# FFN2's down projection: the eleventh pair of inner tiles goes through the seven products as well, and the output is stored block by block

## The chip, the cores and the metric

The kernel runs on one core of a Trainium2 chip. The metric is the device time of one execution in microseconds. The core's engines work side by side, each through its own list of instructions in order: TensorE (PE in the profile, its weight loads PEld), VectorE (DVE), ScalarE (ACT), GpSimd (POOL) and SyncE (SP, its DMA queue SPq). All transfers of this kernel are issued by SyncE.

## The reference

One layer of a decoder trunk: a half-step SwiGLU feed-forward (FFN1), a mixing block of two attentions, and a second half-step SwiGLU (FFN2). Only the last one matters here:

```python
def swiglu(x, w_gate, w_up, w_down):
    return (jax.nn.silu(x @ w_gate) * (x @ w_up)) @ w_down

x = x + FFN_RESIDUAL_WEIGHT * swiglu(rms_norm(x, ffn2_norm[l]),
                                     ffn2_w_gate[l], ffn2_w_up[l], ffn2_w_down[l])
```

There are 1024 tokens, the model width is 1024, the hidden width is 2816, and the factor is 0.5. The last product is therefore [1024, 2816] by [2816, 1024], in float32.

## The kernel before

The hidden width is cut into 22 inner tiles of 128. Each float32 operand is split into a high and a low part (ScalarE casts, line 159, and VectorE subtracts, line 160), and a float32 product is three matmuls: high by high, high by low, low by high.

FFN2's down projection (`ffn_down`) takes inner tiles in pairs. A pair gives a 2x2 block product: two halves of the tokens by two inner tiles, times two inner tiles by two halves of the output columns. Instead of eight products of halves, seven are made (Winograd's form of Strassen's method); the operands of some are sums of blocks. The sums of activations are made on GpSimd by `act_sums` (lines 526 to 529, four sums for a pair of tiles) and stored by line 531 to the DRAM tensor `sumd`, eight blocks of 128 x 512 for a pair. The sums of w_down are made on GpSimd when a pair of its tiles has been loaded: three in `weights` (lines 702 to 704), and one more (line 741) while the second product is prepared.

Ten of the eleven pairs, inner tiles 2 to 21, go this way (`KT` is 10). They are worked off in two halves of `CK` = 5 pairs. The list `steps` has for each half the seven products and for each product its five pairs: 70 steps of 4 x 3 = 12 matmuls (line 760), one for each token tile of 128 tokens and part. Between the steps of one product the result is accumulated in PSUM, in one of two sets of four banks (`one` and `banks`). The four banks of `banks` lie in two PSUM tiles of two banks each. After the last step of a product, VectorE adds its four results to x in SBUF (line 768). Operands are prepared three steps ahead, in a ring of eight buffers, which is four steps.

Activations are fetched by line 715 into buffers of the tag `u`: one fetch for the first three pairs of a product (768 KB), one for the other two (512 KB). The tag has eight buffers; x holds four, so four are left for fetches. The last call of `act_sums` for pair 10 (`pending`) is made at step 5.

The first pair, inner tiles 0 and 1, is treated directly after all steps: for each of the eight token tiles and both halves of the columns 2 x 3 matmuls into a PSUM tile of one bank (lines 153 to 155, called at the end of `ffn_down`), an addition to x (line 788), and then `tail2` stores the token tile, 512 KB in one piece, the last one in two halves (line 243). Its operands are loaded and split during the last products (lines 772 to 777).

The order of each engine's instructions is set by a scheduler that works on the program as written and on priorities; it also decides in which order buffers are given out. What the queue of SyncE holds is worked off strictly in that order: an instruction that waits holds all behind it.

FFN1 uses the same function with another `tail`.

Of the kernel before, what the change touches and what calls it, by code (L numbers as in the profile page):

```python
# [9 lines left out]
F32 = mybir.dt.float32  # L10
# [7 lines left out]
P = 128  # L18
T = 1024
NT = T // P  # L20
D = 1024
# [42 lines left out]
class Layer:  # L64
# [108 lines left out]
    def layer(self):  # L173
        src = self.i["x"][0]
        x = self.parts("v", NT, 2)
        tags = dict(t1=("wd", "wd"), t2=("v", "v"), t3=("wd", "wd"), t4=("v", "act"), w="act", e=("u", "u", "act"))
        norm = self.norm_begin(x, None, ("u", "u"), raw="v", sums=tags)
        self.load_x(x, src, range(1))
        norm["g"] = self.gain("ffn1_norm")
        self.load_x(x, src, range(1, 4))  # L180
        loads = self.ffn_loads("ffn1", 0)
        self.load_x(x, src, range(4, NT))
        self.constants()
        first = self.start(norm, loads)
        mix = self.norm_begin(None, None, ("u", "u"), spill=self.xd)
        lat = {}
        held = []

        def tail(t):
            if t < 0:  # L190
                mix["g"] = self.gain("mix_norm")
                lat["w"] = self.in_weights("lat", None)
                return
            parts = self.norm_parts(mix, t)
            parts[0]()
            held.append(parts[1:])
            if t >= 1:
                for f in held.pop(0):
                    f()
            if t >= 2:  # L200
                self.lat_tile(lat["w"], mix, t - 2)

        pending = self.ffn_up(norm, "ffn1", first, tags)
        x = self.parts("act", NT, 2)
        mix["x"] = x
        self.load_x(x, src, range(NT))
        self.ffn_down(x, "ffn1", dict(raw=("u", "u"), extra="v", acts="wd"), tail, pending)
        self.constants2()
        for parts in held:
            for f in parts:  # L210
                f()
        for t in range(NT - 2, NT):
            self.lat_tile(lat["w"], mix, t)
        hT = mix["hi"], mix["lo"]
        gates = []
        self.in_proj(hT, gates)
        first = self.attention(gates)
        ws = []
        mixed = self.branch_fox(first, lambda: ws.append(self.wo_weights(0, "u")))
        x = self.parts("u", NT, 2)  # L220
        self.load_x(x, self.xd, range(NT))
        ws.append(self.wo_weights(1, "v"))
        tags = dict(t1=("v", "v"), t2=("u", "u"), t3=("v", "v"), t4=("u", "u"), w="u", e=("wd", "wd", "u"))
        norm2 = self.norm_begin(x, self.gain("ffn2_norm"), ("act", "wd"), spill=self.xd2, raw="u", sums=tags)
        first = [self.col_split(l) for l in self.ffn_loads("ffn2", 0)]
        for n in range(2):
            for t in range(4):
                self.w_o(x, mixed, ws, t, n)
        for t in range(4, NT):
            for n in range(2):  # L230
                self.w_o(x, mixed, ws, t, n)
            self.norm_tile(norm2, t - 4)
        first = self.first_half(norm2, first, [self.norm_parts(norm2, t) for t in range(4, NT)])

        pending = self.ffn_up(norm2, "ffn2", first, tags)
        x = self.parts("u", NT, 2)
        self.load_x(x, self.xd2, range(NT))

        def tail2(t):
            if t >= 0:  # L240
                cut = (0, HALF, D) if t == NT - 1 else (0, D)
                for e, f in zip(cut, cut[1:]):
                    self.nc.sync.dma_start(self.out[0][t * P:(t + 1) * P, e:f], x.at(t, slice(e, f)))

        self.ffn_down(x, "ffn2", dict(raw=("act", "wd"), extra="v", acts="u"), tail2, pending)

    def start(self, norm, loads):
        ET = mybir.EngineType
# [59 lines left out]
    def constants(self):  # L308
        nc = self.nc
        c = self.cst  # L310
        self.ident = c.tile([P, P], F32, name="ident")
        make_identity(nc, self.ident)
        self.eps = c.tile([P, 1], F32, name="eps")
        nc.gpsimd.memset(self.eps, EPS)
        warm = self.sm.tile([P, 1], F32, tag="ss", bufs=4, name="warm")
        nc.scalar.activation(warm, self.eps, AF.Abs_reciprocal_sqrt)
        d = self.dram
        self.xd = d.tile([T, D], F32, name="xd")
        self.xd2 = d.tile([T, D], F32, name="xd2")

        self.actd = [d.tile([2, P, T], F32, name=f"actd{k}") for k in range(2)]
        self.sumd = [d.tile([8, P, KT, HALF], F32, name=f"sumd{k}") for k in range(2)]
        self.latd = d.tile([NT, P, LATW], F32, name="latd")
        self.ad = d.tile([HEADS, 4, T], F32, name="ad")
        self.bd = d.tile([HEADS, 4, T], F32, name="bd")
        self.gd = d.tile([2, KD, P, T], F32, name="gd")
        self.fd = d.tile([2, 2, 4, P, T], F32, name="fd")
        self.mn = d.tile([2, 2, HEADS, HD, T], F32, name="mn")
        self.mr = d.tile([2, HEADS, RD, T], F32, name="mr")
        self.mk = d.tile([2, RD, T], F32, name="mk")  # L330
        self.vd = d.tile([2, NT, P, HEADS * P], F32, name="vd")
        self.rd = d.tile([2, 4, 2, T], F32, name="rd")
        self.atd = d.tile([2, 4, P, T], F32, name="atd")
# [341 lines left out]
    def ffn_down(self, x, name, tags, tail, pending):  # L675

        nc = self.nc  # L680
        wd = self.i[f"{name}_w_down"][0]
        sums, src = self.sumd[name == "ffn2"], self.actd[name == "ffn2"]
        CK = KT // 2

        order = (
            (0, "b11", 0, 0), (4, "b21", 0, 0), (6, "t2", 0, 1), (3, "t1", 1, 1),
# [2 lines left out]
        raw, extra, staged = {}, {}, {}  # L689

        def weights(k):
            if k >= KT or k in raw:
                return
            w = self.slot(tags["raw"][k % 2]).rearrange("p (k d n) -> p k d n", k=2, d=2)
            for h in range(2):
                r = (2 + 2 * k + h) * P
                nc.sync.dma_start(w[:, h], wd[r:r + P, :].rearrange("p (d n) -> p d n", d=2))
            if k % CK % 2 == 0:
                extra[k] = self.slot(tags["extra"]).rearrange("p (k s n) -> p k s n", k=2, s=2)
            e = extra[k - k % CK % 2][:, k % CK % 2]  # L700
            v = nc.gpsimd.tensor_tensor
            v(out=e[:, 1], in0=w[:, 1, 1], in1=w[:, 0, 1], op=ALU.subtract)
            v(out=w[:, 0, 1], in0=w[:, 0, 1], in1=w[:, 0, 0], op=ALU.subtract)
            v(out=e[:, 0], in0=w[:, 1, 1], in1=w[:, 0, 1], op=ALU.subtract)
            raw[k] = dict(
                b11=w[:, 0, 0], b21=w[:, 1, 0], t1=w[:, 0, 1], b22=w[:, 1, 1], t2=e[:, 0], t3=e[:, 1], t4=w[:, 1, 0],
            )

        def acts(c, i, k):

            if (c, i, k) in staged:
                return staged[c, i, k]
            n = min(3, CK - k)
            st = self.slot(tags["acts"]).rearrange("p (k n) -> p k n", n=HALF)
            nc.sync.dma_start(st[:, :n], sums[order[i][0], :, c * CK + k:c * CK + k + n, :])
            for j in range(n):
                staged[c, i, k + j] = st[:, j]
            return staged[c, i, k]

        steps = [(c, i, k) for c in range(2) for i in range(7) for k in range(CK)]  # L720

        def operand(src):
            tag = ("stg", "whi", "wlo", "atp")[self.opn % 4]
# [5 lines left out]
        def prep(n):  # L729
# [4 lines left out]
                weights(c * CK + k)  # L734
            if c == 0 and i == 4:
                weights(CK + k)
            w = raw[c * CK + k]
            a = operand(acts(c, i, k))
            b = operand(w[order[i][1]])
# [6 lines left out]
        for n, (c, i, k) in enumerate(steps):  # L746
# [5 lines left out]
            ready.append(prep(n + ahead))  # L752
            if n == CK:
                pending()
            (ah, al), (wh, wl) = ready.pop(0)
            start = i in (0, 1, 3) and k == 0
            for q, o in enumerate(sets[i % 2]):
                r = slice(q * P, (q + 1) * P)
                for m, (u, w) in enumerate(((ah, wh), (ah, wl), (al, wh))):
                    nc.tensor.matmul(  # L760
                        o, lhsT=u[:, r], rhs=w, start=start and m == 0, stop=k == CK - 1 and m == 2,
                        skip_group_check=True,
                    )
            if k == CK - 1:
                _, _, th, dh = order[i]
                for q, o in enumerate(sets[i % 2]):
                    xt = x.at(4 * th + q, slice(dh * HALF, (dh + 1) * HALF))
                    nc.vector.scalar_tensor_tensor(out=xt, in0=o, scalar=0.5, in1=xt, op0=ALU.mult, op1=ALU.add)
            if (c, i, k) == (1, 5, CK - 1):
                both = []  # L770
                for d in (src, wd):
                    hi, lo = (self.slot(tags["extra"], F32R).rearrange("p (j n) -> p j n", j=2) for _ in range(2))
                    for j in range(2):
                        st = self.slot(tags["acts"])[:, :T]
                        nc.sync.dma_start(st, src[j] if d is src else wd[j * P:(j + 1) * P, :])
                        self.split_sb(hi[:, j, :], lo[:, j, :], st)
                    both.append((hi, lo))
        tail(-1)
        (ah, al), (wh, wl) = both
        for t in range(NT):  # L780
# [815 lines left out]
```

## Time and profile before

| | us |
|---|---|
| median of 3 runs | 2142.39 (2140.18 to 2144.15) |
| the profiled execution's own time | 2143.52 |
| its span, from the first to the last instruction | 2141.6 |
| PE busy | 2109.0 |
| DVE busy | 1299.1 |
| first matmul of FFN2's down projection | 1923.4 |
| first and last matmul of its direct part | 2116.0 and 2137.6 |

Times in the profile are counted from the start of the span. A row of the timeline gives the start, the duration, the engine, the line, the operation, what it writes and reads, how many instructions are merged in the row, and in brackets how long the engine stood idle before it and what ended that. Matmuls are pipelined: each has a duration of 0.39 us, but the next begins earlier. A row of the table of windows gives for a stretch its length, the busy time and count of PE, PEld, DVE, ACT and POOL, the granted TensorE clock, the share of the DMA engines that was busy and the GB/s that they moved. In a row of DMA issues stand the size of one and the median time from issue to landing.

### The profile page before, as it was taken

Reading aid. Unit: us, or ns where it says so; the run is one execution under the profiler, and the core shown is the slowest. Engines: PE = TensorE matmul, PEld = TensorE weight load, DVE = VectorE, ACT = ScalarE, POOL = GpSimd, SP = SyncE. Lnnn points to the kernel's source line nnn. Section 1 sums busy time; section 2 is a strip of 40 time slices with the busy share of each in tenths; the row PEclk is TensorE's granted clock in tenths of the full one; section 3 lists DMA queues with packets and bytes.
Section 4 is the critical chain, followed back from the end, with each engine's and each line's share of the span. In section 5 each row is a group of like instructions: output and inputs, shape, how many; then the busy total and the mean of one; then the engine's idle time right before and its main releaser. Section 6 shows DMA issues by size and latency. Waiting matters only on the chain.

```text
span 2141.6 us, 27835 instructions
## 1 busy us (share of the span) xinstructions
PE 2109.0 (98%) x10113; PEld 1761.4 (82%) x10113; DVE 1299.1 (61%) x2054; ACT 946.9 (44%) x1757; POOL 717.7 (34%) x719
## 2 busy tenths in 40 slices
PE   7999999999999999999999999999999999999999
PEld 6888888878888878888888888888888888887887
DVE  7644444468775787545656677753844444449765
ACT  6333333334444554356656675422533333334442
POOL 0564555563201111123333432000355545546200
PEclk8999999999999999999999999999999999999999
DMA  6143333475424377575555783642232434266432
GB/s 172 54 138 99 93 124 99 137 266 183 133 97 159 98 219 207 195 188 138 143 139 141 185 219 115 210 154 73 75 98 79 138 99 137 80 228 238 134 107 108
DMA packets 251633, 305.36 MB, mean 143 GB/s; under 512 B 17656, under 2 KB 186472, under 8 KB 251496
## 3 DMA queue, kind: packets, MB, share of 16 engines
q1 hardware_dynamic: 251496, 303.59, 45.8%
q8 instruction: 79, 1.29, 0.3%
q14 instruction: 58, 0.48, 0.1%
HBM read 205.54 MB, written 98.00 MB: 142 GB/s over the span
## 4 chain that ended last, share of the span: by engine, by line
PE 90%; DVE 4%; DMA 2%; ACT 2%; issue 1%; SPq 0%; POOL 0%; DVEq 0%; ACTq 0%; POOLq 0%
PE pst L620 20%; PE psd L760 16%; PE psb L620 11%; PE psg L620 4%; PE pss L1379 4%; PE pspt L1405 3%; PE pspv L1416 3%; PE psgate L153 3%; PE psgate L155 3%; PE psgate L154 3%; PE psb L155 2%; PE psb L154 2%; PE psb L153 2%; PE psin L153 2%; PE psin L155 2%; PE psin L154 2%
## 5 line engine op out<-in xcount | busy, mean ns | idle before, releaser
L760 PE MATMUL psd<-op 128*128 128x512 f32 x1680 | 382.1, 389 | 1.6 <-DVE op L160 1.6
L760 PEld LDWEIGHTS psd<-op 128*128 128x128 f32 x1680 | 315.5, 188 | 67.9 <-DVE op L160 2.5
L160 DVE TENSOR_TENSOR op<-s_u,op 128x512 fp32r<-128x512 f32 x220 | 198.7, 906 | 113.8 <-ACT op L159 113.2
L159 ACT CAST op<-s_u 128x512 fp32r<-128x512 f32 x220 | 136.1, 621 | 218.0 <-PE psd L760 92.5
L620 PE MATMUL pst<-s_u,op 128*128 128x512 f32 x720 | 173.1, 389 | 0.8 <-DVE s_wd L662 0.8
L620 PE MATMUL pst<-s_v,op 128*128 128x512 f32 x640 | 169.0, 391 | 3.3 <-DVE s_u L662 3.3
L160 DVE TENSOR_TENSOR op<-s_act,op 128x512 fp32r<-128x512 f32 x125 | 114.3, 917 | 77.3 <-ACT op L159 77.0
L620 PEld LDWEIGHTS pst<-s_u,op 128*128 128x128 f32 x720 | 135.1, 188 | 29.2 <-DVE s_wd L662 1.2
L620 PEld LDWEIGHTS pst<-s_v,op 128*128 128x128 f32 x640 | 120.7, 189 | 28.8 <-DVE s_u L662 3.7
L1386 ACT ACTIVATE s_act<-pss,nm 128x128 f32<-128x128 f32 (+7 forms) x128 | 95.0, 743 | 98.7 <-DVE nm L1383 97.8
L596 POOL TENSOR_TENSOR sums<-s_u 128x512 f32<-128x512 f32 x20 | 28.0, 1402 | 319.8 <-DVE wlo L435 176.3
L159 ACT CAST op<-s_act 128x512 fp32r<-128x512 f32 x125 | 77.5, 622 | 110.2 <-PE pst L620 55.6
L1379 PE MATMUL pss<-s_wd 96*128 96x256 f32 (+5 forms) x480 | 112.7, 361 | 0.0
L160 DVE TENSOR_TENSOR op<-sums,op 128x512 fp32r<-128x512 f32 x80 | 60.0, 750 | 86.8 <-ACT op L159 86.3
L1424 DVE TENSOR_TENSOR cmb<-pspv,cmb 64x512 f32<-64x512 f32 x64 | 44.1, 688 | 103.6 <-ACT cmb L1423 103.2
L160 DVE TENSOR_TENSOR op<-s_wd,op 128x512 fp32r<-128x512 f32 x95 | 83.1, 879 | 38.7 <-ACT op L159 38.6
L153 PE MATMUL psgate<-s_u,whi 128*128 128x512 f32 x256 | 101.7, 397 | 0.3 <-ACT z L1228 0.3
L155 PE MATMUL psgate<-s_u,wlo 128*128 128x512 f32 x256 | 100.6, 393 | 1.3 <-POOL wlo L435 1.3
L1409 DVE TENSOR_TENSOR s_v<-pspt,s_v 128x512 fp32r<-128x512 f32 (+1 forms) x160 | 96.3, 631 | 7.6 <-ACT s_v L1408 5.9
L154 PE MATMUL psgate<-s_u,whi 128*128 128x512 f32 x256 | 100.8, 394 | 0.0
L159 ACT CAST op<-s_wd 128x512 fp32r<-128x512 f32 x95 | 58.6, 621 | 91.6 <-PE psd L760 89.7
L1426 POOL COPY atp<-cmb 64x128 f32<-64x128 f32 x64 | 18.4, 287 | 227.5 <-DVE cmb L1424 227.2
(506 smaller groups left out, 4899.4 us busy)
## 6 DMA issues: line engine op xcount, KB each, us to landing
sumd<-s_u SPq DMA_DIRECT2D x20, 1024.0 KB, 4.2
sumd<-s_wd SPq DMA_DIRECT2D x13, 1024.0 KB
s_wd<-fd SPq DMA_DIRECT2D x48, 256.0 KB, 5.5
s_u<-in_ffn_w_down_dram SPq DMA_DIRECT2D x22, 512.0 KB, 6.3
s_wd<-sumd SPq DMA_DIRECT2D x14, 768.0 KB, 4.2
s_u<-sumd SPq DMA_DIRECT2D x14, 768.0 KB, 4.4
s_act<-in_ffn_w_gate_dram SPq DMA_DIRECT2D x20, 512.0 KB, 3.9
s_act<-in_ffn_w_up_dram SPq DMA_DIRECT2D x20, 512.0 KB
```

The lines of the kernel that those rows point to most:

```text
L153: mm(out, lhsT=lh, rhs=rh, start=start, stop=False)
L154: mm(out, lhsT=lh, rhs=rl, start=False, stop=False)
L155: mm(out, lhsT=ll, rhs=rh, start=False, stop=stop)
L159: self.nc.scalar.copy(hi, src)
L160: self.nc.vector.tensor_tensor(out=lo, in0=src, in1=hi, op=ALU.subtract)
L620: mm(out, lhsT=a[:, k, :], rhs=b[:, k, :], start=start and k == 0 and i == 0, stop=k == n - 1 and i == 2, skip_group_check=True,)
L760: nc.tensor.matmul(o, lhsT=u[:, r], rhs=w, start=start and m == 0, stop=k == CK - 1 and m == 2, skip_group_check=True,)
L1379: mm(ps[:, b:e], lhsT=a[:, q], rhs=bb[:, b:e], start=k == 0, stop=k == len(passes) - 1)
L1386: nc.scalar.activation(pn[:, :n], ps[:, :n], AF.Exp, bias=nm, accum_out=rs[:, i, j:j + 1])
L1405: nc.tensor.transpose(pt[:, o:o + P], pr[m][:, kt * P:(kt + 1) * P], self.ident)
L1409: nc.vector.tensor_tensor(out=lo, in0=pt[:, s0:], in1=hi, op=ALU.subtract)
L1416: mm(po[:, :256], lhsT=v[:, kt, :], rhs=slabs[c // 2][:, s, c % 2, e * 256:(e + 1) * 256], start=kt == 0 and s == 0, stop=False,)
```

## The change

The direct part of FFN2 is gone: its call passes no tail, and `ffn_down` then counts eleven pairs, five in the first half and six in the second (`count`), 35 + 42 = 77 steps. The sums of the first pair's activations, which are stored as `actd` in DRAM, are made at step 5 directly behind `pending`: two buffers of the tag `u` are loaded, `act_sums` makes the four sums, and both are stored to the new DRAM tensor `sum0`. In the second half each product has a sixth step, whose activations are fetched from `sum0` by a DMA of their own. Its tiles of w_down are loaded and summed like the others, from the fifth product of the first half on.

The result is stored when a block of 512 tokens by 512 columns is complete, after products 1, 4, 5 and 6 of the second half, in four stores of 256 KB. The last three steps are written token tile by token tile: for each, the nine matmuls of the three steps, the addition and the store.

FFN1 keeps its direct part. Its instructions are the same as before, and everything ahead of FFN2's down projection stands in the same order on all engines.

```diff
-        def tail2(t):
-            if t >= 0:
-                cut = (0, HALF, D) if t == NT - 1 else (0, D)
-                for e, f in zip(cut, cut[1:]):
-                    self.nc.sync.dma_start(self.out[0][t * P:(t + 1) * P, e:f], x.at(t, slice(e, f)))
-
-        self.ffn_down(x, "ffn2", dict(raw=("act", "wd"), extra="v", acts="u"), tail2, pending)
+        self.ffn_down(x, "ffn2", dict(raw=("act", "wd"), extra="v", acts="u"), None, pending)
...
+        self.sum0 = d.tile([8, P, HALF], F32, name="sum0")
...
+        count = (CK, KT - CK + (tail is None))
+        total = sum(count)
...
-            if k >= KT or k in raw:
+            if k >= total or k in raw:
                 return
+            pos = k if k < CK else k - CK
...
-                r = (2 + 2 * k + h) * P
+                r = (2 + 2 * k + h) % NH * P
...
-            n = min(3, CK - k)
+            n = min(3, count[c] - k)
             st = self.slot(tags["acts"]).rearrange("p (k n) -> p k n", n=HALF)
-            nc.sync.dma_start(st[:, :n], sums[order[i][0], :, c * CK + k:c * CK + k + n, :])
+            m = min(n, KT - c * CK - k)
+            nc.sync.dma_start(st[:, :m], sums[order[i][0], :, c * CK + k:c * CK + k + m, :])
+            if m < n:
+                nc.sync.dma_start(st[:, m], self.sum0[order[i][0]])
...
-        steps = [(c, i, k) for c in range(2) for i in range(7) for k in range(CK)]
+        steps = [(c, i, k) for c in range(2) for i in range(7) for k in range(count[c])]
...
+            if (c, i, k) == (0, 5, 0):
+                weights(KT)
...
             if n == CK:
                 pending()
+                if tail is None:
+                    pair = [self.slot(tags["acts"]).rearrange("p (s n) -> p s n", s=4) for _ in range(2)]
+                    for j, e in enumerate(pair):
+                        nc.sync.dma_start(e[:, :2], src[j].rearrange("p (s n) -> p s n", s=2))
+                    self.act_sums(*pair, self.sum0)
...
+            def add(q):
+                xt = x.at(4 * th + q, cols)
+                nc.vector.scalar_tensor_tensor(
+                    out=xt, in0=sets[i % 2][q], scalar=0.5, in1=xt, op0=ALU.mult, op1=ALU.add
+                )
+
+                if tail is None and c == 1 and i in (1, 4, 5, 6):
+                    t = 4 * th + q
+                    nc.sync.dma_start(self.out[0][t * P:(t + 1) * P, cols], xt)
+
+            if tail is None and n >= len(steps) - ahead:
+
+                if n == len(steps) - ahead:
+                    for q in range(4):
+                        for e in range(ahead):
+                            part(q, k + e, ready[e])
+                        add(q)
+                continue
```

SyncE's queue around the place where the first pair's sums are made. Before, behind the two stores of `pending`; the fetches from `sumd` are, in this order, those of steps 10 to 12, 13 and 14, 15 to 17, and 18 and 19 (a step's number counts from 0; in brackets stands which semaphores are waited for, `Pool` and `DVE` being the engines' and `DMAHW` those of transfers):

```order
L531 DMA sumd1_104<-s_u_16030 128x4x512 [waits Pool_49]
L531 DMA sumd1_104<-s_wd_16160 128x4x512 [waits DMAHW1_49,Pool_49]
L715 DMA s_u_16492<-sumd1_104 128x1536 [waits DMAHW3_49,DMAHW2_49,DVE_49]
L715 DMA s_u_16552<-sumd1_104 128x1024 [waits DMAHW6_49,DVE_49]
L715 DMA s_u_16590<-sumd1_104 128x1536 [waits DMAHW4_49,DMAHW0_49]
L715 DMA s_u_16650<-sumd1_104 128x1024 [waits DMAHW7_49,DMAHW5_49,DVE_49]
```

The same place in the changed kernel (its lines are numbered anew: 527 is the store in `act_sums`, 716 the fetch, 763 the load of the first pair):

```order
L527 DMA sumd1_104<-s_u_16031 128x4x512 [waits Pool_49]
L527 DMA sumd1_104<-s_wd_16161 128x4x512 [waits DMAHW1_49,Pool_49]
L763 DMA s_u_16462<-actd1_102 128x1024 [waits DMAHW3_49,DMAHW2_49,DVE_49]
L763 DMA s_u_16463<-actd1_102 128x1024 [waits DMAHW6_49,DVE_49]
L716 DMA s_u_16503<-sumd1_104 128x1536 [waits DMAHW4_49,DMAHW0_49]
L527 DMA sum0_105<-s_u_16462 128x4x512 [waits DMAHW5_49,DMAHW2_49,Pool_49]
L527 DMA sum0_105<-s_u_16463 128x4x512 [waits DMAHW3_49,Pool_49]
L716 DMA s_u_16563<-sumd1_104 128x1024 [waits DMAHW7_49,DVE_49]
L716 DMA s_u_16601<-sumd1_104 128x1536 [waits DMAHW4_49,DVE_49]
L716 DMA s_u_16661<-sumd1_104 128x1024 [waits DMAHW5_49,DMAHW1_49]
```

The two loads of the first pair stand where the fetches of steps 10 to 12 and of 13 and 14 stood; the fetch of 13 and 14 now stands behind the stores to `sum0`.

GpSimd's list at the same place in the changed kernel (746 is the fourth sum of w, 522 to 525 are the sums of `act_sums`, 702 the first sum of the next pair of w):

```order
L746 TENSOR_TENSOR s_wd_16333<-s_wd_16333,s_v_16317 128x512 [waits DVE_49]
L746 TENSOR_TENSOR s_act_16359<-s_act_16359,s_v_16362 128x512 [waits DVE_49,Pool_49]
L522 TENSOR_TENSOR s_u_16462<-s_u_16462 128x512 [waits DMAHW3_49,DMAHW2_49,PE_49]
L523 TENSOR_TENSOR s_u_16462<-s_u_16462,s_u_16463 128x512 [waits DMAHW3_49]
L524 TENSOR_TENSOR s_u_16463<-s_u_16462 128x512 [waits DMAHW6_49,PE_49,Pool_49]
L525 TENSOR_TENSOR s_u_16463<-s_u_16463 128x512 [waits Pool_49]
L702 TENSOR_TENSOR s_v_16702<-s_wd_16699 128x512 [waits DMAHW3_49,DMAHW2_49]
```

The four new sums stand behind the last sum for the first half's w; in the list before, line 702 follows it directly.

TensorE's last rows in the changed kernel (773 is the matmul of a step; `psd_17092` holds the first and second token tile of the block, `psd_17093` the third and fourth):

```order
L773 MATMUL psd_17092<-op_17860,op_17857 128x512 [waits DVE_49]
L773 MATMUL psd_17092<-op_17860,op_17857 128x512
L773 MATMUL psd_17093<-op_17824,op_17821 128x512 x3
L773 MATMUL psd_17093<-op_17842,op_17839 128x512
L773 MATMUL psd_17092<-op_17824,op_17821 128x512 [waits DVE_49]
L773 MATMUL psd_17092<-op_17824,op_17821 128x512 x2
L773 MATMUL psd_17092<-op_17842,op_17839 128x512 x3
L773 MATMUL psd_17092<-op_17860,op_17857 128x512 x3
L773 MATMUL psd_17093<-op_17842,op_17839 128x512 x2
L773 MATMUL psd_17093<-op_17860,op_17857 128x512 x3
L773 MATMUL psd_17093<-op_17824,op_17821 128x512 [waits DVE_49]
L773 MATMUL psd_17093<-op_17824,op_17821 128x512 x2
```

Where before each token tile of the last product's steps was worked in turn and the direct part followed in PSUM tiles of their own, four matmuls of the third token tile stand between the first and the second, and the second and the fourth begin with a wait for VectorE.

More of the change, by code (lines that the diff above doesn't have):

```diff
@@ L691, in weights @@
         def weights(k):
-            if k >= KT or k in raw:
+            if k >= total or k in raw:
                 return
+            pos = k if k < CK else k - CK
             w = self.slot(tags["raw"][k % 2]).rearrange("p (k d n) -> p k d n", k=2, d=2)
             for h in range(2):
-                r = (2 + 2 * k + h) * P
+                r = (2 + 2 * k + h) % NH * P
                 nc.sync.dma_start(w[:, h], wd[r:r + P, :].rearrange("p (d n) -> p d n", d=2))
-            if k % CK % 2 == 0:
+            if pos % 2 == 0:
                 extra[k] = self.slot(tags["extra"]).rearrange("p (k s n) -> p k s n", k=2, s=2)
-            e = extra[k - k % CK % 2][:, k % CK % 2]
+            e = extra[k - pos % 2][:, pos % 2]
             v = nc.gpsimd.tensor_tensor
@@ L754, in ffn_down @@
                 pending()
-            (ah, al), (wh, wl) = ready.pop(0)
-            start = i in (0, 1, 3) and k == 0
-            for q, o in enumerate(sets[i % 2]):
+                if tail is None:
[3 more added lines that the diff above has]
+                    self.act_sums(*pair, self.sum0)
@@ L758, in ffn_down, with part @@
+            _, _, th, dh = order[i]
+            cols = slice(dh * HALF, (dh + 1) * HALF)
+            def part(q, k, ops):
+                (ah, al), (wh, wl) = ops
                 r = slice(q * P, (q + 1) * P)
+                start = i in (0, 1, 3) and k == 0
                 for m, (u, w) in enumerate(((ah, wh), (ah, wl), (al, wh))):
                     nc.tensor.matmul(
-                        o, lhsT=u[:, r], rhs=w, start=start and m == 0, stop=k == CK - 1 and m == 2,
-                        skip_group_check=True,
-                    )
@@ L764, in ffn_down @@
[L764 to L769, printed above, removed]
+                        sets[i % 2][q], lhsT=u[:, r], rhs=w, start=start and m == 0,
+                        stop=k == count[c] - 1 and m == 2, skip_group_check=True,
+                    )
@@ L770, in ffn_down @@
+            ops = ready.pop(0)
+            for q in range(4):
+                part(q, k, ops)
+            if k == count[c] - 1:
+                for q in range(4):
+                    add(q)
+            if tail is not None and (c, i, k) == (1, 5, CK - 1):
                 both = []
@@ L777, in ffn_down @@
                     both.append((hi, lo))
+        if tail is None:
+            return
         tail(-1)
```

## The prediction

> **What bounds the kernel now.** I read the busy times first, then the chain that ended last, then the down projection of FFN2 (from 1923 us on) instruction by instruction.
>
> ```profile
> PE 2109.0 (98%) x10113; PEld 1761.4 (82%) x10113; DVE 1299.1 (61%) x2054; ACT 946.9 (44%) x1757; POOL 717.7 (34%) x719
> PE 90%; DVE 4%; DMA 2%; ACT 2%; issue 1%; SPq 0%; POOL 0%; DVEq 0%; ACTq 0%; POOLq 0%
> 1947.47 168.71 PE psd L760 x743
> ```
>
> TensorE is the bound: 98% busy, 90% of the chain. The third row is the chain inside the changed stage: 743 matmuls without a break, 168.71 / 743 = 0.227 us each, so a step of twelve takes 2.72 us. There, a matmul less is 0.227 us less, and any operand that comes late is added in full. Where can operands be late? The stage's first part answers:
>
> ```profile
> 1923.40 14.21 PE L760 MATMUL psd<-op 128*128 128x512 f32 x62
> 1938.78 8.23 PE L760 MATMUL psd<-op 128*128 128x512 f32 x35 [1.16 <-DVE op L160]
> 1947.47 12.76 PE L760 MATMUL psd<-op 128*128 128x512 f32 x55 [0.47 <-DVE op L160]
> 1946.74 0.68 DVE L160 TENSOR_TENSOR op<-s_wd,op 128x512 fp32r<-128x512 f32 x1
> 1947.94 1.78 DVE L160 TENSOR_TENSOR op<-s_act,op 128x512 fp32r<-128x512 f32 x1
> 1949.87 1.61 POOL L741 TENSOR_TENSOR s_act<-s_act,s_v 128x512 f32<-128x512 f32 x1 [0.70 <-DVE op L160]
> 1950.25 2.38 DVE L160 TENSOR_TENSOR op<-s_u,op 128x512 fp32r<-128x512 f32 x2
> ```
>
> Here VectorE ends last. A split (L160) takes 0.68 us alone, but 1.78 us beside a GpSimd sum, so that while GpSimd works a step's two splits take some 3.4 us against TensorE's 2.72. It stops twice, 1.16 and 0.47 us, and then never again. The second stop ends with the split of w in step 8 (1946.74 + 0.68), on which the second matmul of step 8 waited; counted on from it, the third matmul of step 13, 61 later, starts at 1947.47 + 61 x 0.227 = 1961.3 us. (Step n is the nth of the stage's 70, from 0; step 13 is the third product with the fourth pair.)
>
> **Matmuls.** The direct part's 8 x 2 x 2 x 3 = 96 become 7 x 4 x 3 = 84.
>
> ```profile
> 2116.01 0.39 PE L153 MATMUL psb<-s_v 128*128 128x512 f32 x1
> 2137.55 0.39 PE L155 MATMUL psb<-s_v 128*128 128x512 f32 x1
> ```
>
> These are the first and last of the 96: 21.54 / 95 = 0.227 us, the same pace, and both parts use a new weight load for each matmul. So 12 x 0.227 = **-2.72 us**, the whole gain. VectorE loses 16 of its 72 additions to x and gains six splits net (eight go, fourteen come), ScalarE gains six casts.
>
> ```profile
> 2020.16 2.47 DVE L768 SCALAR_TENSOR_TENSOR s_u<-psd,s_u 128x512 f32<-128x512 f32 x4
> ```
>
> That is the addition of a whole product, 2.47 us, now once in six steps of the second half: with two splits, 2 x 0.68 + 2.47 / 6 = 1.8 us a step lie under TensorE's 2.72 wherever GpSimd rests.
>
> **The pair's sums, and the queue behind them.** GpSimd makes four more sums, after those of w, and their tiles take two of the four buffers through which activations are fetched. SyncE's one queue now holds, in this order, the two loads, one fetch, two stores that need the sums, and only then the fetch for steps 13 and 14.
>
> ```profile
> 1926.34 1.63 POOL L527 TENSOR_TENSOR s_u<-s_u,s_wd 128x512 f32<-128x512 f32 x1
> 1928.05 1.62 POOL L528 TENSOR_TENSOR s_wd<-s_u 128x512 f32<-128x512 f32 x1
> 1929.75 1.62 POOL L529 TENSOR_TENSOR s_wd<-s_wd 128x512 f32<-128x512 f32 x1
> 1931.40 0.37 SPq L531 DMA_DIRECT2D sumd<-s_wd  x1
> 1942.15 0.81 SPq L715 DMA_DIRECT2D s_u<-sumd  x2
> 1953.01 0.62 ACT L159 CAST op<-s_u 128x512 fp32r<-128x512 f32 x1 [1.58 <-PE psd L760]
> ```
>
> The first four rows are the same work for the pair before: one sum every 1.70 us beside VectorE, the second store 0.03 us behind the last sum. The two fetches at 1942.15 us are of steps 13 and 14 and of the three after; the cast of step 13 came at 1953.01 us, so its data lay ready. In the changed kernel the second load takes the buffer free at 1942.15. GpSimd's last sum for w ends at 1949.87 + 1.61 = 1951.5 us in both; four sums follow, to 1951.5 + 3 x 1.70 + 1.62 = 1958.2; the second store is issued then and the fetch for step 13 behind it, at 1958.6 us, 16 us later than now. When does that land?
>
> ```profile
> sumd<-s_u SPq DMA_DIRECT2D x20, 1024.0 KB, 4.2
> s_act<-in_ffn_w_gate_dram SPq DMA_DIRECT2D x20, 512.0 KB, 3.9
> s_u<-sumd SPq DMA_DIRECT2D x1, 768.0 KB, 9.9
> 1938.00:1940.00 2.00, 1.22 (x5) 1.05 (x6) 2.00 (x2) 0.34 (x1) 2.00 (x3) 1.00 1.00 411
> 1914.98 6.99 DMA s_u<-sumd
> 1921.99 0.63 ACT op L159
> 1922.64 1.11 DVE op L160 x2
> ```
>
> A load of 512 KB lands 3.9 us after its issue, the store of 1 MB 4.2 us; with all engines busy 411 GB/s move. If the load starts at once it lands at 1962.5; if it moves behind the store, at 1958.2 + 4.2 + 0.52 MB / 411 GB/s (1.3) = 1963.7. The 9.9 us are those of a fetch issued right after such a store while 15 us of transfers were queued; as the far bound they give 1968.5. I take 1963.7: that row shows waiting in line, and the line is one store long here. A landing is followed by cast and split (last rows): 0.02 + 0.62 + 0.03 + 0.69 = 1.4 us, and TensorE takes up 0.2 us behind a split (below): landing + 1.6. The third matmul of step 13 then starts at 1965.3 instead of 1961.3: **+4.0 us** (2.8 to 8.8). The new sums also slow the splits of steps 10 to 12: step 10's is done some 0.8 us late, but time lost before step 13 only shortens the wait there.
>
> [...] No row here shows a lone store with a lone load behind it.
>
> What is late next?
>
> ```profile
> 1976.81 1.30 POOL L702 TENSOR_TENSOR s_v<-s_wd 128x512 f32<-128x512 f32 x1 [10.54 <-DVE op L160]
> 2006.25 1.55 POOL L702 TENSOR_TENSOR s_v<-s_act 128x512 f32<-128x512 f32 x1 [24.55 <-DMA s_act<-in_ffn_w_down_dram]
> 2014.37 1.62 POOL L704 TENSOR_TENSOR s_v<-s_wd 128x512 f32<-128x512 f32 x1
> 2018.95 0.69 DVE L160 TENSOR_TENSOR op<-s_u,op 128x512 fp32r<-128x512 f32 x1 [0.61 <-ACT op L159]
> ```
>
> TensorE restarts with step 14 ready, and the next sums on GpSimd need loads of w that come behind the fetches, 0.79 + 0.52 + 1.05 MB later (5.7 us); the third of these three pairs has to wait for its buffer, as now (first row). So I count no further stop, but see the first rival. In the second half three pairs' sums follow each other instead of two. Now (rows two to four) the six sums run to 2016.0 us, and 3 us later VectorE waits for ScalarE again, so it has caught up; one pair more slows three more splits by 1.1 us each, under a lead of three steps. The seven loads of the first pair's sums cost 0.3 us of the queue each, and the stores of finished blocks stand in it behind fetches made twelve steps ahead: nothing is late there.
>
> **The end.** The last three steps run token tile by token tile. Two token tiles lie in one PSUM tile, and the order shows the matmuls of the second and fourth waiting for VectorE: for the addition of the tile before.
>
> ```profile
> 2137.09 0.39 PE L153 MATMUL psb<-s_v 128*128 128x512 f32 x1
> 2136.61 0.69 DVE L788 SCALAR_TENSOR_TENSOR s_u<-psb,s_u 128x512 f32<-128x512 f32 x1 [0.67 <-PE psb L155]
> 2137.97 0.69 DVE L788 SCALAR_TENSOR_TENSOR s_u<-psb,s_u 128x512 f32<-128x512 f32 x1 [0.67 <-PE psb L155]
> 1919.76 0.69 DVE L662 TENSOR_TENSOR s_wd<-pst,s_wd 128x512 f32<-128x512 f32 x1 [0.64 <-PE pst L620]
> 1920.51 3.06 PE L620 MATMUL pst<-s_u,op 128*128 128x512 f32 x12 [0.78 <-DVE s_wd L662]
> 1908.68 2.88 PE L620 MATMUL psb<-s_v,op 128*128 128x512 f32 x12
> 2137.33 1.69 SPq L243 DMA_DIRECT2D out_dram<-s_u  x2
> ```
>
> The addition starts 2137.97 - 2137.55 = 0.42 us after the start of the last matmul and takes 0.69. From VectorE's end at 1920.45 to TensorE's start pass 0.06 us, and these twelve matmuls took 3.06 - 2.88 = 0.18 more: 0.24. So the next matmul of that PSUM tile comes 0.42 + 0.69 + 0.24 = 1.35 us after the last one's start, not 0.23. The second token tile has four other matmuls put ahead of it (0.91): 0.2 us lost. The fourth has none: 1.1 us lost. **+1.3 us**, between nothing (if a wait is for something long past) and 2.2. After the last matmul both kernels have one addition and one store of 256 KB, issued behind the last of one row above: no difference.
>
> **Sum.** -2.72 + 4.0 + 1.3 = +2.6 us. The profiled execution, 2143.52 us (span 2141.6), would become 2146.1; it lies 1.13 above the median of the runs, so the forecast is 2142.39 + 2.6 = **2145.0 us**: no change that a measurement can tell, since about 0.2% (4.3 us) is the least that counts.
>
> **Rivals.** *VectorE stays behind after the restart.* TensorE restarts with a lead of one step, and GpSimd has six sums of w to make. If they start while the lead is below some 4.5 us, six sums cover three steps: 3 x (3.4 - 2.72) = 2.0, and the four additions of a product, 2.4 us, fall among them: +4.5, in all +7.1: 2149.5 us, slower. For it: at 1938 and 1947 us just this stopped TensorE. Against: by the transfer times the first of these sums starts 5.7 us after step 13's data, when VectorE, at two splits per 1.36 us where its data lie ready, is three steps ahead.
>
> *The queue's wait is covered.* If the sums run free of VectorE, or the scheduler's order has the fetch's data earlier than I think, step 13 loses nothing: -2.72 + 1.3: 2141.0 us. For it: all data moved easily before (the two fetches waited 10 us unused). Against: the stores stand ahead of the fetch and need the last sum, 3 us before step 13.
>
> *The end's waits cost nothing.* Then 2145.0 - 1.3 = 2143.7. [...] Against it stands only the order's wait.
>
> **How the numbers follow.** Both waits as worked out 0.57; VectorE behind after the restart 0.18; the queue's wait covered 0.15; no loss at the end 0.10. The likeliest gives 2145.0. Downward the range takes in the covered wait (2141.0, 0.5 below for the runs' scatter), upward a landing of 1967.2, between the store's line and the far bound: 2140.5 to 2148.5. Faster than 2138.1 needs, beyond the covered waits, a gain that no row shows: 0.08, mostly out of the second rival. Slower than 2146.7 takes the first rival and a landing after 1965.4, about a sixth of the first case: 0.28. Within: 0.64.
>
> **What would show it.** In the changed profile: 924 matmuls instead of 936 in the stage; the sum0 stores at about 1955 and 1958 us and the fetch directly behind; one stop of TensorE of about 4 us near 1961, ended by a split whose cast waited for a DMA; then no stop to the last product; a stop of 1.1 us some 2.5 us before the last matmul. It is wrong if TensorE stops more than once between 1964 and 1985 (first rival), if step 13 starts on time (second), or if the fetch lands much after its store.

## The result, and the profile after

| | before | after |
|---|---|---|
| median of 11 runs, us | 2142.98 (2140.18 to 2144.22) | 2147.32 (2144.62 to 2148.61) |
| ratio, 95% interval | | 1.0022 [1.0014, 1.0029] |
| span of the profiled execution, us | 2141.6 | 2145.7 |
| first matmul of the changed stage, us | 1923.40 | 1921.78 |
| from there to the end of the span, us | 218.2 | 223.9 |

The changed kernel is slower by 4.3 us (0.22%, between 0.14 and 0.29%). The predicted 2145.0 us was 2.3 us too low. The time lies inside the range, and the sign of the sum was right, but the likeliest case, "no change that a measurement can tell", was missed by a hair: the result is just beyond 0.2%.

The last row of the table is the one to compare by. Everything ahead of the changed stage is the same in both kernels and still differs by some us between executions, and the table of windows shows where. Its columns are the length, the busy time and count of PE, the granted TensorE clock, the busy share of the DMA engines and GB/s. The first fence is of the kernel before, the second of the one after:

```profile
0.00:100.00 100.00, 86.82 (x405) 0.91 0.42 121
...
1918.00:2133.00 215.00, 212.59 (x935) 1.00 0.44 152
```

```profile
0.00:100.00 100.00, 87.18 (x411) 0.95 0.42 121
...
1918.00:2133.00 215.00, 208.55 (x904) 0.98 0.48 170
```

In the first 100 us the clock was granted at 0.91 in one execution and at 0.95 in the other, which puts the changed kernel 1.5 us ahead there. Further differences of 0.5 to 2.1 us, in both directions, follow up to 1430 us; at the stage all of them add up to the 1.6 us between the two starts, and they have nothing to do with the change. The last row of each is a stretch that covers most of the changed stage: 935 matmuls before 2133 us have become 904, and the clock is below 1.00 here, which it was not before.

Now the timeline of TensorE in the stage after the change (the columns are those of the prediction's second fence):

```profile
1921.78 14.21 PE L773 MATMUL psd<-op 128*128 128x512 f32 x62
1937.16 8.23 PE L773 MATMUL psd<-op 128*128 128x512 f32 x35 [1.16 <-DVE op L160]
1945.85 5.96 PE L773 MATMUL psd<-op 128*128 128x512 f32 x25 [0.47 <-DVE op L160]
1952.17 8.02 PE L773 MATMUL psd<-op 128*128 128x512 f32 x34 [0.36 <-DVE op L160]
1963.86 175.11 PE L773 MATMUL psd<-op 128*128 128x512 f32 x759 [3.68 <-ACT op L159]
2139.76 2.35 PE L773 MATMUL psd<-op 128*128 128x512 f32 x9 [0.78 <-DVE s_u L780]
```

The counts add up to 924. The first two stops are those of before. New are a short one (0.36 us), the long one of 3.68 us ahead of step 13, and one of 0.78 us near the end. Between the last two, 759 matmuls run without a break. What ended the long stop is told by the timelines of GpSimd and of SyncE's queue, and by the chain that ended last (start, length, what):

```profile
1948.25 1.62 POOL L746 TENSOR_TENSOR s_act<-s_act,s_v 128x512 f32<-128x512 f32 x1 [0.69 <-DVE op L160]
1949.82 1.74 POOL L522 TENSOR_TENSOR s_u<-s_u 128x512 f32<-128x512 f32 x1
1955.04 1.62 POOL L525 TENSOR_TENSOR s_u<-s_u 128x512 f32<-128x512 f32 x1
1953.28 3.77 SPq L527 DMA_DIRECT2D sum<-s_u  x2
1957.14 2.70 SPq L716 DMA_DIRECT2D s_u<-sumd  x3
```

```profile
1957.14 6.03 DMA s_u<-sumd
...
1963.86 175.13 PE psd L773 x759
```

The four sums of the pair follow directly on the last sum of w (1948.25 us) and end at 1955.04 + 1.62 = 1956.66. The two stores (fourth row) hold the queue until 0.4 us later (1957.05), and the fetch for step 13 is issued right behind them. That is 35.4 us into the stage; the prediction had 1958.6 - 1923.4 = 35.2. It landed 6.03 us after its issue, where the prediction took 5.1; 0.69 us later the first matmul of step 13 started.

Something else lies in the 759 matmuls. The windows of this kernel around the stop:

```profile
1962.00:1963.00 1.00, 0.00 (x0) 0.74 1.10 453
1963.00:1964.00 1.00, 0.14 (x1) 0.50 0.99 399
1964.00:1969.00 5.00, 5.00 (x12) 0.50 1.02 418
1969.00:1970.00 1.00, 1.00 (x5) 0.85 1.03 414
1970.00:1975.00 5.00, 5.00 (x24) 1.00 1.02 409
```

TensorE had fallen idle at 1952.17 + 8.02 = 1960.2 us. The granted clock went to 0.50 at 1962.5 (0.74 in the first row is the mean over that us) and stayed there until 1969.3. In the five us from 1964 on 12 matmuls began, in the five from 1970 on 24. TensorE lost time twice: while it stood, and after that at half speed.

### The profile page after: what moved, and what is told of

Read it like the earlier page. It is cut to its first block, busy times and chain, and to the rows that moved or that the text cites. A ratio compares the mean times of both kernels' runs of the same rounds, so it can differ in the third digit from the quotient of the medians.

```text
span 2145.7 us, 27860 instructions
## 1 busy us (share of the span) xinstructions
PE 2110.0 (98%) x10101; PEld 1759.4 (82%) x10101; DVE 1302.6 (61%) x2048; ACT 951.4 (44%) x1767; POOL 734.2 (34%) x727
## 4 chain that ended last, share of the span: by engine, by line
PE 90%; DVE 4%; DMA 3%; ACT 2%; issue 1%; SPq 1%; POOL 0%; ACTq 0%; DVEq 0%; POOLq 0%
PE pst L616 20%; PE psd L773 17%; PE psb L616 11%; PE psg L616 4%; PE pss L1414 4%; PE pspt L1440 3%; PE pspv L1451 3%; PE psgate L153 3%; PE psgate L155 3%; PE psgate L154 3%; PE psb L155 2%; PE psb L154 2%; PE psb L153 2%; PE psin L153 2%; PE psin L154 2%; PE psin L155 2%
## 5 line engine op out<-in xcount | busy, mean ns | idle before, releaser
L773 PE MATMUL psd<-op 128*128 128x512 f32 x1764 | 404.6, 391 | 6.4 <-ACT op L159 3.7
L773 PEld LDWEIGHTS psd<-op 128*128 128x128 f32 x1764 | 332.5, 189 | 78.1 <-ACT op L159 4.1
L160 DVE TENSOR_TENSOR op<-s_u,op 128x512 fp32r<-128x512 f32 x227 | 205.7, 910 | 128.7 <-ACT op L159 128.1
L160 DVE TENSOR_TENSOR op<-s_act,op 128x512 fp32r<-128x512 f32 x130 | 122.7, 945 | 77.2 <-ACT op L159 76.7
```

What stands on the lines that cost most here:

```text
L160: self.nc.vector.tensor_tensor(out=lo, in0=src, in1=hi, op=ALU.subtract)
L773: nc.tensor.matmul(sets[i % 2][q], lhsT=u[:, r], rhs=w, start=start and m == 0, stop=k == count[c] - 1 and m == 2, skip_group_check=True,)
```

## The experiments

Each was timed beside the kernel before on the same chip. The first four shared one set of runs of it (median 2141.85 us of 33), the last four another (2142.48 of 30). In the diffs the left side is the changed kernel. Since run medians of this kernel tell apart no less than about 2 us, each kernel is also read by its stage, from the first matmul of step 0 to the end of the span.

### The stores out of the fetch's way

The stores of the pair's sums are issued from GpSimd's queue, so that SyncE's fetch for step 13 stands behind nothing that needs the sums.

```diff
-    def act_sums(self, a, b, dst):
+    def act_sums(self, a, b, dst, queue=None):
-            self.nc.sync.dma_start(dst[s:s + 4].rearrange("s p n -> p s n"), e)
+            (queue or self.nc.sync).dma_start(dst[s:s + 4].rearrange("s p n -> p s n"), e)
-                    self.act_sums(*pair, self.sum0)
+                    self.act_sums(*pair, self.sum0, self.nc.gpsimd)
```

> The two stores of the first pair's sums are issued by GpSimd itself instead of SyncE; nothing else is changed. The profile of the changed kernel has three losses in the stage: the first matmul of step 13 comes 4.6 us late (1963.9 us where the step's place is 1959.2), behind a fetch issued at 1957.1 us after those stores; then the granted clock is 0.5 for the 5.4 us from 1963.9 to 1969.3, which costs 2.7 us; and two stops at the end cost 1.2 us. Theory A (the queue): the fetch only stands behind stores that wait for GpSimd. Without them in SyncE's queue it is issued near 1948 us, step 13 starts in time, the clock stays at 1.0, and the time is 2147.3 - 4.2 - 2.7 = 2140.4 us (0.4 us of late splits at step 10 stay), about 0.9990 of before. Theory B (the buffers): the first pair's two tiles take two of four fetch buffers, here for as long as before, so that some fetch is late anyway; the stop stays or moves to step 15 or 18 and the time stays near 2147.

Measured: 2146.56 us, ratio 1.0019 [1.0011, 1.0028]. The wait for data was gone: the cast for step 13, first row of this timeline, could run at 1952.33 us. And yet TensorE stopped:

```profile
1952.33 0.62 ACT L159 CAST op<-s_u 128x512 fp32r<-128x512 f32 x1 [1.58 <-PE psd L773]
1956.38 2.28 DVE L160 TENSOR_TENSOR op<-s_v,op 128x512 fp32r<-128x512 f32 x1
1958.58 2.47 DVE L780 SCALAR_TENSOR_TENSOR s_u<-psd,s_u 128x512 f32<-128x512 f32 x4
1960.98 1.44 DVE L160 TENSOR_TENSOR op<-s_u,op 128x512 fp32r<-128x512 f32 x1
1962.35 1.75 DVE L160 TENSOR_TENSOR op<-s_v,op 128x512 fp32r<-128x512 f32 x1
1961.95 1.59 POOL L704 TENSOR_TENSOR s_v<-s_wd 128x512 f32<-128x512 f32 x1
1964.15 173.95 PE L773 MATMUL psd<-op 128*128 128x512 f32 x758 [2.42 <-DVE op L160]
```

VectorE works without a gap. The splits of step 13 (rows four and five) take 1.44 and 1.75 us beside GpSimd, which goes straight on to the next sums of w (1959.20 to 1963.54 us, where in the changed kernel it had nothing to do until 1970.50); alone they take 0.68. Part of this the edit itself makes: issuing the two stores takes 0.93 and 0.77 us of GpSimd's time, and the split that runs meanwhile (second row) takes 2.28 us instead of the 1.78 of the changed kernel. The second matmul of step 13 starts 1964.15 - 1922.68 = 41.5 us into the stage instead of 37.7: 3.8 us late, with the data long there. Behind the queue stood a second limit that was nearly as late. "The queue's wait is covered" therefore does not lead, by this edit, to the 2141.0 us that the prediction had for it.

### The clock

Sixteen matmuls that nobody uses, written into PSUM banks that hold nothing at that point, fill the wait ahead of step 13.

```diff
+            if tail is None and (c, i, k) == (0, 2, 2):
+                for m in range(16):
+                    nc.tensor.matmul(
+                        sets[1][m % 4], lhsT=ops[0][0][:, :P], rhs=ops[1][0], start=True, stop=True,
+                        skip_group_check=True,
+                    )
```

> 16 matmuls that are not needed are put behind step 12, into the PSUM banks that the fourth product clears when it starts; the fetch stays as late as it is. They fill 16 x 0.227 = 3.6 us of the wait before step 13. Theory A (the clock): the matmuls after the wait are slow because TensorE stood still; with it kept busy the granted clock stays at 1.0 and the time falls by 2.7 us to 2144.6, although TensorE has more to do. Theory B: the matmuls after the wait are slow because of the transfers and the sums beside them; then they stay slow, and the time is 2147.3 or a little more.

Measured: 2146.50 us, ratio 1.0020 [1.0011, 1.0028]; the 2144.6 us of theory A did not show, and against the changed kernel's ratio this tells nothing at these intervals. The profile does, by its timeline and its windows:

```profile
1961.81 3.79 PE L801 MATMUL psd<-op 128*128 128x512 f32 x16
1965.67 172.83 PE L773 MATMUL psd<-op 128*128 128x512 f32 x759
```

```profile
1962.00:1966.00 4.00, 3.92 (x17) 1.00 1.01 359
1966.00:1970.00 4.00, 4.00 (x18) 1.00 1.02 414
```

Step 13 starts as late as before (42.4 us into the stage, after the change 42.1), but the clock stays at 1.00, and the same 759 matmuls take 172.83 us instead of 175.11. So the half clock cost **2.3 us** in the profiled execution of the changed kernel, and it comes from TensorE's standing still, not from the load on the DMA engines, which is as high here (1.02 in the last row, 1.02 at half clock in the changed kernel).

### The order at the end

The last three steps take the token tiles in the order 0, 2, 1, 3, so that two tiles which follow each other lie in different PSUM tiles.

```diff
-                    for q in range(4):
+                    for q in (0, 2, 1, 3):
```

> The last three steps go through the token tiles in the order 0, 2, 1, 3, so that each follows one of the other PSUM tile. Theory A: the stops at the end are waits for the addition of the token tile before in the same PSUM tile; both vanish, 1.2 us less: 2146.1. Theory B: TensorE waits there for something else, or the end is set by the stores: the stops stay and the time stays at 2147.3.

Measured: 2146.61 us, ratio 1.0020 [1.0011, 1.0029]. Timeline, then windows:

```profile
1965.36 176.27 PE L773 MATMUL psd<-op 128*128 128x512 f32 x768 [3.71 <-ACT op L159]
```

```profile
1966.00:1967.00 1.00, 1.00 (x4) 0.85 1.06 436
...
1970.00:1971.00 1.00, 1.00 (x6) 0.94 1.00 406
```

759 and 9 matmuls have become one stretch of 768: no stop near the end. Here too the clock fell to 0.50: from 1966.7 to 1970.1 us, which begins 1.3 us after the matmuls had started again. What the end costs is read from a clean pair of kernels below.

### Both at once

The edits of the first and the third experiment together.

> The edits of the first and the third run together: stores of the first pair's sums from GpSimd's queue, token tiles at the end in the order 0, 2, 1, 3. If the losses are the three named, what is left is the twelve matmuls fewer, -2.72 us, and 0.4 us of late splits: 2143.0 - 2.3 = 2140.7 us, 0.9989 of before. If the two edits remove the same time, it stays at the better of the two alone.

Measured: 2144.25 us, ratio 1.0008 [0.9999, 1.0017]. Expected was 0.9989; TensorE still waits for VectorE, as in the first experiment. Timeline, then windows:

```profile
1962.06 174.15 PE L773 MATMUL psd<-op 128*128 128x512 f32 x767 [2.43 <-DVE op L160]
```

```profile
1962.00:1965.00 3.00, 2.94 (x13) 1.00 0.95 315
1965.00:1968.00 3.00, 3.00 (x15) 1.00 0.87 289
```

The stop is that of the first experiment to 0.01 us, but the clock stays at 1.00. In the first experiment it had fallen after the matmuls had begun again, as its windows show:

```profile
1964.00:1965.00 1.00, 0.85 (x4) 0.95 1.03 418
1965.00:1968.00 3.00, 3.00 (x9) 0.50 0.88 240
1968.00:1969.00 1.00, 1.00 (x5) 0.84 0.73 252
```

### The changed kernel again

The same kernel as in the result, to see what in its stage repeats.

> The changed kernel itself, beside the others on one chip. All theories: 1.002 of before, as measured already; one long stop of TensorE before step 13. If the drop of the clock depends on more than the length of the stop, its place and length will differ from those of the first profile (0.5 from 1963.9 to 1969.3 us).

Measured: 2147.06 us, ratio 1.0024 [1.0014, 1.0034]. The long stop is there again, the stretch at half clock is not the same (timeline, then windows):

```profile
1964.11 174.10 PE L773 MATMUL psd<-op 128*128 128x512 f32 x759 [3.82 <-ACT op L159]
```

```profile
1964.00:1965.00 1.00, 0.89 (x2) 0.57 0.93 379
...
1967.00:1968.00 1.00, 1.00 (x5) 0.72 1.04 426
```

This time the clock fell with the restart and was back at 1967.6 us: 174.10 - 172.83 = 1.3 us lost instead of 2.3.

### Short sums

What makes the stores late: GpSimd's time, or the transfers themselves? Here the pair's sums are made over 16 of their 512 columns. The other columns keep what a second load of the same tile put there, so this kernel leaves out nearly all of the pair's sums, while the stores, their waits and their order stay.

```diff
+        whole = a, b
+        if dst is self.sum0:
+            a, b = a[:, :, :16], b[:, :, :16]
-        for e, s in ((a, 0), (b, 4)):
+        for e, s in zip(whole, (0, 4)):
-                        nc.sync.dma_start(e[:, :2], src[j].rearrange("p (s n) -> p s n", s=2))
+                        for s in (0, 2):
+                            nc.sync.dma_start(e[:, s:s + 2], src[j].rearrange("p (s n) -> p s n", s=2))
```

> The four sums of the first pair are made over 16 of 512 columns (the rest of the result is left as loaded, so the output differs); order, buffers, loads, stores and waits are as in the changed kernel. With the stores moved to GpSimd's queue the fetch was in time, and yet TensorE stopped for 2.4 us before the second matmul of step 13, for a split of VectorE. Theory A (GpSimd's time): the sums' 6.8 us both hold the queue and slow VectorE's splits. Without them the fetch for step 13 is issued near 1951 instead of 1957.1, its splits run at 0.68 us, and there is no stop near step 13 and no drop of the clock: 2147.3 - 4.6 - 2.7 = 2140.0 us, 0.9987 of before. Theory B (the queue's order and the buffers): stores and fetches stand as before, so a stop of over 2 us stays, and the time stays above 2144.

Measured: 2142.29 us, ratio 1.0004 [0.9995, 1.0013], between what the two theories gave. GpSimd, SyncE's queue and TensorE:

```profile
1948.29 0.22 POOL L528 TENSOR_TENSOR s_u<-s_u 128x16 f32<-128x16 f32 x1
1949.00 3.77 SPq L719 DMA_DIRECT2D s_u<-sumd  x3
1957.91 172.83 PE L777 MATMUL psd<-op 128*128 128x512 f32 x759 [0.80 <-ACT op L159]
```

The fetch goes out 1949.00 - 1918.61 = 30.4 us into the stage, 5.0 us earlier than after the change, and the stop shrinks from 3.68 to 0.80 us; the clock does not fall. So it is GpSimd's 6.8 us of sums that hold the queue. The transfers have a share too: the two stores are now issued within 1 us (1947.93 to 1948.90), so that both, 2 MB, are ahead of the fetch; it takes 8.2 us to land, and step 13 is still 1.8 us late.

### The sums later

Instead of directly behind `pending` at step 5, the pair is loaded, summed and stored at step 20. Nothing reads it before the second half, step 35 and later.

```diff
             if n == CK:
                 pending()
+            if n == 4 * CK:
                 if tail is None:
```

> The first pair's loads, sums and stores are made at step 20 instead of step 5, nothing else is changed. GpSimd has been idle for some time there, VectorE is three steps ahead, and the fetch behind the stores is that of steps 25 to 27: issued near 1984, landed near 1989, due near 1991. Theory A: no stop, no drop of the clock, only the two stops at the end stay: -2.72 + 1.2 = -1.5 us, 0.9993 of before. Theory B (two of four buffers are missed wherever it is put): a stop of 2 us or more near step 25, above 2143.

Measured: 2140.04 us, ratio 0.9990 [0.9982, 0.9999]. Timeline of TensorE, SyncE's queue and ScalarE:

```profile
1945.20 185.90 PE L774 MATMUL psd<-op 128*128 128x512 f32 x818 [0.42 <-DVE op L160]
2131.89 2.37 PE L774 MATMUL psd<-op 128*128 128x512 f32 x9 [0.79 <-DVE s_u L781]
1979.19 16.79 SPq L716 DMA_DIRECT2D s_u<-sumd  x6
1986.26 0.62 ACT L159 CAST op<-s_u 128x512 fp32r<-128x512 f32 x1 [4.42 <-DMA s_u<-sumd]
```

No stop in the middle: 818 matmuls in one stretch. The fetch behind the two stores, here one of 768 KB, takes 7.1 us to land (last two rows), but it meets engines that are ahead: ScalarE waits 4.42 us for it, TensorE does not. The same sums, stores and wait in the queue cost TensorE nothing at this place.

### The sums later, and the order at the end

The last edit and that of the order at the end, together.

> The sums at step 20 as in the run before, and the token tiles of the last three steps in the order 0, 2, 1, 3. If the waits are all named, what remains is the twelve matmuls fewer: -2.7 us, 0.9987 of before. If the addition of the tile before isn't what TensorE waits for at the end, as much as the run before: 0.9993.

Measured: 2138.89 us, ratio **0.9985 [0.9977, 0.9994]**: faster than both kernels, by little. From the second matmul of step 8 to the last of the stage there is one row:

```profile
1942.30 187.75 PE L774 MATMUL psd<-op 128*128 128x512 f32 x827 [0.47 <-DVE op L160]
```

187.75 / 827 = 0.227 us, the pace of before. The stage takes 2133.7 - 1918.21 = 215.5 us, 2.7 less than before: the twelve matmuls, and nothing else. Against the kernel above, which differs by the order at the end alone, it is 216.6 - 215.5 = 1.1 us shorter. The first stops of the stage are not the same in these two executions (0.99 us there, 1.19 here). From the second matmul of step 8 to the end of the last matmul, where these stops have no part, it is 2131.89 + 2.37 - 1945.20 = 189.06 us there and 187.75 here: the order at the end is worth 1.3 us.

## Why the prediction was right or wrong

The stages of all kernels, taken apart by the prediction's terms. "Step 13" is how much later than before the first matmul behind the stop starts, counted from the start of the stage (before, it is 59 matmuls behind 1947.47 us: 1960.9, 37.5 into the stage; in the first and fourth experiment the second matmul, 37.7). At the pace of the last kernel (187.75 / 827) 759 matmuls would take 172.3 us, and they took 172.83 without a fall of the clock. Of these 0.5 us, 0.2 is the second token tile's wait at the end (the 818 matmuls of "later", which do not start behind a cast, are 0.2 over that pace too); the other 0.3 is the restart, in which the next matmuls still wait for splits, and is added to "Step 13" where the stop ended with a cast. "Clock" is what is then left over in the time of the matmuls behind the stop. "End" is the 1.3 us of the clean pair, and is not measured as a whole in the others.

| kernel | stage, us | against before | matmuls | step 13 | clock | end | sum |
|---|---|---|---|---|---|---|---|
| after | 223.9 | +5.7 | -2.7 | +4.9 | +2.3 | +1.3 | +5.8 |
| after, again | 223.3 | +5.1 | -2.7 | +5.2 | +1.3 | +1.3 | +5.1 |
| stores on GpSimd's queue | 222.3 | +4.1 | -2.7 | +3.8 | +1.7 | +1.3 | +4.1 |
| wait filled | 222.0 | +3.8 | -2.7 | +5.2 | 0 | +1.3 | +3.8 |
| order at the end | 222.0 | +3.8 | -2.7 | +4.9 | +1.6 | 0 | +3.8 |
| stores and order | 219.3 | +1.1 | -2.7 | +3.8 | 0 | 0 | +1.1 |
| short sums | 219.0 | +0.8 | -2.7 | +2.1 | 0 | +1.3 | +0.7 |
| later | 216.6 | -1.6 | -2.7 | 0 | 0 | +1.3 | -1.4 |
| later, and order | 215.5 | -2.7 | -2.7 | 0 | 0 | 0 | -2.7 |

Each stage is one execution. That the sums close says less than it seems: "step 13" and "clock" are read off the same stage, and only the matmuls and the end come from elsewhere. What tests the terms is that each goes to 0 in the kernel from which its cause was taken. In "later" the 0.2 us that are left are its shorter first stop. The ratios of the runs put the kernels in nearly the same order.

**Matmuls, -2.72.** Right, and shown alone in the last kernel of the table.

**The fetch behind the stores, +4.0.** The mechanism, its place and the moment of issue (35.2 forecast, 35.4 measured) were right; the stop near 1961 us stands where it was put. The term was too small by 0.9 us: the landing took 6.0 us from the fetch's issue instead of 5.1. Two windows of the changed kernel show where:

```profile
1959.00:1960.00 1.00, 1.00 (x6) 1.00 1.02 283
1960.00:1961.00 1.00, 0.18 (x1) 1.00 0.97 188
```

The line in front of the fetch was one store long, as predicted: by the packets in the trace the store's, of 2 KB, ended at 1961.5 us, and the fetch's, of 4 KB, ran from 1961.0 to 1962.8. But the last two us of the store went at about half pace, 283 and 188 GB/s with all DMA engines busy; a packet took 0.17 us there and 0.087 before. The store thus took 4.8 us instead of the 4.2 of its row, and from the fetch's last packet to its landing passed another 0.4 us. Why the store slowed down is open; it did so in the second execution and with the order at the end too. The far bound, 9.9 us, was not reached.

**The half clock, not in the sum.** This is the step that failed: the prediction priced the stop at its length. In the changed kernel a stop of 3.7 to 3.8 us is followed by half speed for 1.3 to 2.3 us worth of time, and in the profiled execution 2.3, with 0.9 more of landing, is what lies between the forecast of +2.6 and the stage's +5.7. (The medians differ by 4.3; what the clock cost in the executions without a profile is not shown.) Before, no stop in this stage was longer than 1.16 us and its clock was 1.00, so its rows did not show the price. Near 458 us the same trace did show it:

```profile
454.87:458.28 3.41, 1.26 (x5) 1.00 0.25 97
458.28:461.69 3.41, 3.41 (x9) 0.50 0.00 0
```

Behind 3.41 us in which TensorE worked for 1.26, the next 3.41 us ran at a clock of 0.50. So the price could have been read there.

**The end, +1.3.** Right: 1.3 us by the clean pair, with a visible stop of 0.78 us that ends 2 us before the last matmul starts. The rival of no loss at the end did not come true. The wait stood in the program, per PSUM tile of two banks, and it went away when neighbours in time came from different tiles: one stretch of 827 matmuls in "later, and order", where "later" has a stop of 0.79 us.

**No stop after the restart.** Right: 759 matmuls without a break. The rival of VectorE staying behind did not happen there. But its mechanism was real, at another place: once the queue's wait was taken away, the splits beside GpSimd's sums, those of the pair and then those of w, made step 13 late by 3.8 us on their own, the 0.5 us included that the slower split beside the issued stores adds. The prediction had seen those splits late and said that this only shortens the wait at step 13. That is true while the wait lasts, and it means that the second rival, which takes the wait away, was given a price (2141.0) that leaves out what stands behind it. The run that took it away came at 2146.56.

**The range and the chances.** 2140.5 to 2148.5 held 2147.32. The chance of 0.28 for slower than 2146.7 rested on the first rival and on landings after 1965.4 us. Neither came: the landing, 41.4 us into the stage, would be 1964.8 on that scale. What carried the time over 2146.7 was the clock, a term that nobody had counted. That the range held it is luck: its upper part had been put there for something else.

## What to carry to other kernels

An operand that comes late to a busy TensorE costs its delay and, as behind 4 of the 5 stops of 2.42 to 3.82 us here, can also cost a stretch at half clock, worth 1.3 to 2.3 us; price both. When a wait is taken away, look for what would have been late directly behind it: here two limits behind GpSimd's sums made step 13 4.6 and 3.8 us late, and only moving the work to a stretch where everyone was ahead removed both. Work that nothing needs soon should not be issued into a queue, or beside an engine, that has no lead at that moment.

## What the runs showed of the hardware

The granted clock of TensorE fell to 0.50 around four of the five stops of 2.42 to 3.82 us in this stage, at a moment that is not tied to the stop. By the windows shown above it lay at 0.50 from 1962.48 to 1969.30 us in the changed kernel (6.8 us), from 1964.14 to 1967.56 in its other execution, from 1964.90 to 1968.32 behind the stop of 2.42 us, and from 1966.70 to 1970.12 with the order at the end: 3.4 us three times, and twice 3.4. The first fall came 1.38 us before TensorE started again, the others 0.03, 0.75 and 1.34 us after. The stop of 2.43 us in a kernel that differs from the one with 2.42 only at the far end was followed by none. 3.4 us at half speed is 1.7 us of matmuls; the term "clock" is less than that where part of the stretch lay in the stop or in the restart's waits.

The length of the stop is not the whole measure. In the kernel before, TensorE stood for 1.46 us up to 732.61 us, among matmuls of 384 columns and some of 64 rows; at 734.76 us, 2.15 us after it had started again, the clock fell to 0.50 for 3.41 us. The stop of 1.16 us in the stage of that kernel left it at 1.00. What decides between a fall and none stays open here.

Sixteen matmuls that nobody uses, 3.79 us of them, kept the clock at 1.00 through a wait of the same length: the 759 behind it took 172.83 us, against 175.11.
